# DeltaNet scan of a hybrid decoder layer: odd heads one chunk behind the even heads, two sides on opposite halves of the array

## The chip, the cores and the metric

The kernel runs on one core of one Trainium2 chip. A core has TensorE (PE, matrix products; PEld is its weight load), VectorE (DVE), ScalarE (ACT), GpSimd (POOL), SyncE (SP, whose queue issues most loads), a working memory with 128 partitions (rows), and eight accumulator banks (PSUM) that TensorE writes. A matmul that contracts over 64 partitions and writes 64 partitions uses one quarter of TensorE's array: the rows of the array follow the partitions that the operands are read from, its columns those that the result is written to. The metric is the device time of one execution in microseconds.

## What is computed

One decoder layer on 512 tokens with 1024 features, all in float32: normalise, one input projection, three groups of mixers side by side (gated DeltaNet, sparse attention, causal pooling), an output projection, then a squared-ReLU MLP. The change is in the DeltaNet's recurrence. Six heads of 64 features each carry a 64x64 state S over eight chunks of 64 tokens:

```
def step(S, xs):
    u_i, w_i, qk_i, qd_i, kd_i, gl_i = xs
    v_new = u_i - jnp.einsum('bhcd,bhde->bhce', w_i, S)
    o = jnp.einsum('bhcd,bhde->bhce', qd_i, S) + jnp.einsum('bhcs,bhse->bhce', qk_i, v_new)
    S = S * gl_i[..., None, None] + jnp.einsum('bhcd,bhce->bhde', kd_i, v_new)
    return S, o
```

`u` and `w` come from a triangular system per chunk, which the kernel inverts beforehand ("the solve").

## The kernel before

The 512 tokens lie in four tiles (index i) of 128 partitions, so each tile holds two chunks: chunk p=0 on partitions 0 to 63, chunk p=1 on 64 to 127 (`halves[p]`). Five generators are run side by side: `solves` (the systems of tiles 0 and 1 together, then of 2 and 3), `preps`, `slabs` (the input projection, the big 128x256 matmuls of L336), `compress` (L498 to L542) and `scans`. Each yields a cost, and the one that lags most emits next. A scheduler then puts the emitted instructions of each engine in a fixed order. Every engine works through its list in order; PE's list mixes the small matmuls of the solve and the scan with the big ones of the projection, later with attention scores (L983 to L985) and the output projection (L139 to L141 on `hwo`, `lwo`).

The solve (`gdn_solve`, matmuls in `sysmm`, L708) goes in legs: twelve matmuls of 64x64 on PE, one operation on VectorE or ScalarE (L729, L734, L737, later L744 to L762), and the next twelve need its result. `sysmm` alternates p=0 and p=1, so neighbours use opposite quarters of the array; both halves write one tile of one bank.

The scan (`gdn_scan`) takes one chunk per step, all six heads on the same 64 partitions h. A step is five groups of six matmuls: L776 (TT times v) and L779 (minus w times S) into one accumulator tile, L787 (keys times v_new) into the other half of it, and L792 twice (queries times S, QK times v_new). Between them stand L785 (DVE copies v_new), L783 (POOL scales the state), L788 (DVE adds to the new state) and L795 (ACT copies the output out). The scan's accumulator is bank 3 alone, so a step's first matmul comes after the copy of L795 of the step before. `S` is one tile whose half alternates. Steps of tiles 0 and 1 follow the first pair of solves, those of 2 and 3 the second. When all is done `gdn_out` normalises the tiles for the output projection (transposes at L812).

Of the kernel before, what the change touches and what calls it, by code (L numbers as in the profile page):

```python
# [9 lines left out]
F32 = mybir.dt.float32  # L10
# [6 lines left out]
ALU = mybir.AluOpType  # L17
# [20 lines left out]
def trunk_kernel(ctx, tc, x, norm_mix, w_in, conv_w, a_log, dt_bias, gdn_norm, nsa_q_norm, nsa_k_norm,  # L38
                 cmp_pos, cmp_w1, cmp_w2, pool_w, pool_scale, w_out, norm_ffn, w_ffn1, w_ffn2, out):
    nc = tc.nc  # L40
    V, S, G, PE, SY = nc.vector, nc.scalar, nc.gpsimd, nc.tensor, nc.sync
# [29 lines left out]
    pp_, ps_, pc_ = banks(3, 6), banks(3), banks(6)  # L71
# [137 lines left out]
    ps = pn()  # L209
# [401 lines left out]
    gs = gd.enter_context(pool("gs", 1))  # L611
    gte = ExitStack()
    gt = gte.enter_context(pool("gt", 1))
    St = gs.tile([P, H, HD], F32, tag="S", name="S")
    V.memset(St[0:64], 0.0)
    GB = dict(kT=2, D1=2, LT=4, QK=4, qdT=4, tmp=3, gls=1, vn=2, L16=4)
    for a in range(2):
        GB.update({f"X{a}": 1, f"IX{a}": 1, f"TT1{a}": 1, f"T{a}": 5, f"R{a}": 2})

# [5 lines left out]

    def w1t(shape, name, tag=None, dt=F32):
        tag = tag or name
        pl_ = gs if tag in ("LT", "QK", "qdT", "gls", "vn", "tmp") else gt
        return pl_.tile(shape, dt, tag=tag, name=nm(name), bufs=GB[tag])

    def hcol(s_):

        return 2 * (s_ % 3) + s_ // 3

    def v6(ps):
        return ps[:, 0:384].rearrange("p (s c) -> p s c", s=6)
# [132 lines left out]
    def gdn_scan(i):
        d = grp[i]  # L770
        o = vb[:, i]
        for p in range(2):
            h, nh = halves[p], halves[1 - p]
            ps = ps_()
            for s_ in range(6):
                PE.matmul(ps[h, ts(s_, HD)], d["TT"][h, s_], vb[h, i, hcol(s_)], start=(s_ == 0), stop=False,  # L776
                          skip_group_check=True)
            for s_ in range(6):
                PE.matmul(ps[h, ts(s_, HD)], kr[h, i, s_], St[h, hcol(s_)], start=False, stop=(s_ == 5),  # L779
                          skip_group_check=True)  # L780
            yield 0.8
            gls = w1t([P, H, HD], "gls")
            G.tensor_tensor(gls[h], St[h], egc[h, 2, i].unsqueeze(2).to_broadcast([64, H, HD]), ALU.mult)  # L783
            vn = w1t([P, 6, HD], "vn")
            V.tensor_copy(vn[h], v6(ps)[h])  # L785
            for s_ in range(6):
                PE.matmul(ps[nh, ts(hcol(s_), HD)], qr[h, i, hcol(s_)], vn[h, s_], start=True, stop=True)  # L787
            V.tensor_tensor(St[nh], v6(ps)[nh], gls[h], ALU.add)  # L788
            yield 0.4
            for a_ in range(2):  # L790
                for s_ in range(6):
                    PE.matmul(ps[h, ts(hcol(s_), HD)], (d["qdT"][h, s_ // 3, s_ % 3], d["QK"][h, s_])[a_],  # L792
                              (St[h, hcol(s_)], vn[h, s_])[a_], start=(s_ == 0 and a_ == 0), stop=(s_ == 5 and a_ == 1),
                              skip_group_check=True)
# [106 lines left out]

    def scans():
        yield from until("v")
        for ab in ((0, 1), (2, 3)):
            yield from until(ab)
            for i in ab:
                if i == 2:
                    y_tiles((0, 1, 2))
                yield from gdn_scan(i)
                have.add(("s", i))  # L910
# [377 lines left out]
```

## Time and profile before

| what | value |
|---|---|
| median of three runs | 753.72 us (753.46 to 754.56) |
| the profiled execution's own time | 756.4 us |
| span of its instructions | 754.2 us |
| PE busy in the span | 720.5 us (96%) |
| DVE busy | 550.1 us (73%) |
| ACT, POOL busy | 369.2 us, 216.7 us |
| scan, first to last matmul | 182.3 to 304 us of the span |

The profile is of one execution, whose own time is 2.2 us over its span and 2.7 us over the median. PE's busy time is modelled, so 96% busy doesn't say that it does useful work at its best rate for 96% of the time. A float32 matmul appears as two instructions in the trace, here called passes: six matmuls are 12 rows. The granted clock is given as a share of 2.4 GHz: 1.0 is the upper level, 0.5 the lower one of 1.2 GHz.

### The profile page before, as it was taken

The page shows a single profiled execution, that of the slowest core. Times are in us where ns is not written, and L with a number is a line of the kernel's source. Part 1 is how long each engine was busy: PE and PEld are TensorE (multiplying, and loading weights), DVE is VectorE, ACT ScalarE, POOL GpSimd, SP SyncE. Part 2 cuts the span into 40 slices and gives each one's busy share as a digit, 9 for nine tenths or more (in the row PEclk, how much of TensorE's full clock was granted, in tenths as well). Part 3 has the DMA queues.
Part 4 walks back from the last instruction along what each step waited for, and adds up shares of the span by engine and source line. Part 5 has one row for each costly group of instructions (what it writes and reads, how often), then busy time and mean ns, then how long its engine had stood idle before and what let it go on. Part 6 is the DMA issues. An engine that isn't in the chain of part 4 may idle for free.

```text
span 754.2 us, 13267 instructions
## 1 busy us (share of the span) xinstructions
PE 720.5 (96%) x5191; PEld 584.0 (77%) x5191; DVE 550.1 (73%) x1021; ACT 369.2 (49%) x724; POOL 216.7 (29%) x262
## 2 busy tenths in 40 slices
PE   3799989999999999999999999999999999999997
PEld 2788867798899887765557987878788888888886
DVE  5736997879786468667545599796868779686846
ACT  4445654456564235556644555454355444454440
POOL 8335354541514301000002042321405050412323
PEclk9599999999999989999999999999999999999999
DMA  8213321223211053003002042514233331413102
GB/s 268 74 32 84 84 64 45 63 72 104 76 54 30 21 215 102 29 29 118 23 1 85 1 143 81 168 56 141 83 113 111 94 130 44 129 52 112 56 0 111
DMA packets 49921, 62.19 MB, mean 82 GB/s; under 512 B 5494, under 2 KB 42564, under 8 KB 49860
## 3 DMA queue, kind: packets, MB, share of 16 engines
q1 hardware_dynamic: 48144, 60.95, 25.9%
q8 instruction: 40, 0.66, 0.4%
q10 hardware_dynamic: 1716, 0.41, 0.3%
q14 instruction: 21, 0.17, 0.1%
HBM read 59.25 MB, written 2.10 MB: 81 GB/s over the span
## 4 chain that ended last, share of the span: by engine, by line
PE 66%; DVE 21%; DMA 4%; issue 3%; ACT 3%; POOL 2%; SPq 0%; DVEq 0%; ACTq 0%; POOLq 0%
PE ps L139 14%; PE ps L140 14%; PE ps L141 13%; PE ps L336 5%; PE ps L1018 4%; DVE bl L1164 3%; DMA w2r<-in_w_ffn_dram 2%; PE ps L708 2%; DVE x L1257 2%; DVE lw L131 2%; PE ps L1007 2%; PE ps L792 1%; PE ps L983 1%; PE ps L984 1%; PE ps L498 1%
## 5 line engine op out<-in xcount | busy, mean ns | idle before, releaser
L140 PE MATMUL ps<-h2l,hw 128*128 128x512 f32 (+1 forms) x280 | 104.7, 374 | 0.1
L141 PE MATMUL ps<-h2h,lw 128*128 128x512 f32 (+1 forms) x280 | 104.7, 375 | 0.0
L139 PE MATMUL ps<-h2h,hw 128*128 128x512 f32 (+1 forms) x280 | 104.0, 374 | 0.0
L1171 POOL TENSOR_TENSOR al<-gF,ah 128x512 fp32r<-128x512 f32 x24 | 37.7, 1572 | 221.0 <-ACT ah L1170 182.4
L139 PE MATMUL ps<-bh,ah 128*128 128x512 f32 x224 | 88.5, 395 | 2.3 <-DVE x L1257 2.0
L140 PE MATMUL ps<-bl,ah 128*128 128x512 f32 x224 | 88.2, 394 | 0.0
L141 PE MATMUL ps<-bh,al 128*128 128x512 f32 x224 | 84.6, 393 | 0.0
L1257 DVE TENSOR_TENSOR x<-ps,x 128x512 f32<-128x512 f32 x112 | 72.7, 680 | 6.1 <-PE ps L141 5.9
L131 POOL TENSOR_TENSOR lo<-raw,hi 128x512 fp32r<-128x512 f32 (+2 forms) x45 | 60.1, 1349 | 53.5 <-ACT hi L130 49.0
L1164 DVE TENSOR_TENSOR bl<-w2r,bh 128x1024 fp32r<-128x1024 f32 x40 | 57.8, 1446 | 6.3 <-ACT bh L1163 6.3
L1171 POOL TENSOR_TENSOR al<-gS,ah 128x512 fp32r<-128x512 f32 x32 | 53.4, 1687 | 26.0 <-ACT ah L1170 24.7
L140 PEld LDWEIGHTS ps<-h2l,hw 128*128 128x128 f32 x280 | 52.6, 188 | 10.5 <-DVE h2l L1135 0.3
L141 PEld LDWEIGHTS ps<-h2h,lw 128*128 128x128 f32 x280 | 52.5, 188 | 10.2
L139 PEld LDWEIGHTS ps<-h2h,hw 128*128 128x128 f32 x280 | 52.3, 188 | 9.9
L130 ACT CAST hi<-raw 128x512 fp32r<-128x512 f32 (+2 forms) x78 | 39.6, 534 | 30.5 <-DMA raw<-in_w_in_dram 18.1
L1163 ACT CAST bh<-w2r 128x1024 fp32r<-128x1024 f32 x40 | 41.8, 1047 | 24.5 <-PE ps L141 23.5
L139 PEld LDWEIGHTS ps<-bh,ah 128*128 128x128 f32 x224 | 42.0, 188 | 13.5 <-issue 1.8
L141 PEld LDWEIGHTS ps<-bh,al 128*128 128x128 f32 x224 | 42.1, 188 | 9.8
L140 PEld LDWEIGHTS ps<-bl,ah 128*128 128x128 f32 x224 | 42.1, 188 | 9.6
L1170 ACT CAST ah<-gS 128x512 fp32r<-128x512 f32 x32 | 19.7, 620 | 51.6 <-DVE gS L1239 24.4
L131 DVE TENSOR_TENSOR lw<-raw,hw 128x1024 fp32r<-128x1024 f32 x32 | 41.2, 1320 | 4.3 <-ACT hw L130 4.3
L130 ACT CAST hw<-raw 128x1024 fp32r<-128x1024 f32 x32 | 32.1, 1046 | 22.6 <-PE ps L140 22.3
(346 smaller groups left out, 1737.5 us busy)
## 6 DMA issues: line engine op xcount, KB each, us to landing
raw<-in_w_ffn_dram SPq DMA_DIRECT2D x32, 512.0 KB, 4.0
w2r<-in_w_ffn_dram SPq DMA_DIRECT2D x32, 512.0 KB, 5.4
raw<-in_w_in_dram SPq DMA_DIRECT2D x24, 256.0 KB, 2.8
raw<-in_w_in_dram SPq DMA_DIRECT2D x36, 128.0 KB, 2.3
x<-in_x_dram SPq DMA_DIRECT2D x8, 512.0 KB, 5.4
raw<-in_cmp_w_dram SPq DMA_DIRECT2D x32, 128.0 KB, 2.2
raw<-in_w_out_dram SPq DMA_DIRECT2D x8, 512.0 KB, 3.6
out_dram<-x SPq DMA_DIRECT2D x8, 256.0 KB, 2.0
```

The lines of the kernel that those rows point to most:

```text
L130: {"A": S.copy, "V": V.tensor_copy, "G": G.tensor_copy}[e[0]](hi[:, k], r)
L131: {"V": V, "G": G}[e[1]].tensor_tensor(lo[:, k], r, f32v(hi[:, k]), ALU.subtract)
L139: PE.matmul(ps, ah, bh, start=start, stop=False, **kw)
L140: PE.matmul(ps, ah, bl, start=False, stop=False, **kw)
L141: PE.matmul(ps, al, bh, start=False, stop=stop, **kw)
L336: PE.matmul(ps[:, ts(i, 256)], a_[:, k, ts(2 * b + i, P)], w_, start=(k == 0 and n_ == 0 and i == 0), stop=(k == KC - 1 and n_ == 2 and i ...
L1018: PE.matmul(acc[halves[a], i * P:(i + m) * P], Vt[k // 2][:, k % 2, 2 * br + h // 3, :], pt[:, c * P:(c + m) * P], start=False, stop=(br = ...
L1163: S.copy(hi, src)
L1164: V.tensor_tensor(lo, src, f32v(hi), ALU.subtract)
L1170: S.copy(hi, src)
L1171: G.tensor_tensor(lo, src, f32v(hi), ALU.subtract)
L1257: V.tensor_tensor(x2[i][:, cs], acc[bk, t_], x2[i][:, cs], ALU.add)
```

## The change

`gdn_step` takes the place of `gdn_scan`. There are nine steps in place of eight. In step t the even heads (three of them) work on chunk t and the odd heads on chunk t-1, so that the even ones read and write partitions `halves[p]` and the odd ones the other half. Step 0 has the even side alone and step 8 the odd side alone. Within each of the five groups the two sides alternate, matmul by matmul. VectorE's copy and add work on both sides at once: 128 partitions by 192 in place of 64 by 384. POOL's scaling and ScalarE's copy-out are one instruction per side, 64 by 192 each. The state is a new tile each step (three buffers), and the update part of a step stands in columns 192 to 383 of the accumulator tile. The last step updates no state. Step 4 needs the second pair of solves, as the fifth chunk did before, and the odd heads' fourth chunk is in that step too.

```diff
-    St = gs.tile([P, H, HD], F32, tag="S", name="S")
-    V.memset(St[0:64], 0.0)
-    GB = dict(kT=2, D1=2, LT=4, QK=4, qdT=4, tmp=3, gls=1, vn=2, L16=4)
+    GB = dict(kT=2, D1=2, LT=4, QK=4, qdT=4, tmp=3, gls=2, vn=2, S=3, L16=4)
...
+    def gdn_step(t, St):
+
+        sides = []
+        for a in range(2):
+            if 0 <= t - a < 2 * NT:
+                i, p = divmod(t - a, 2)
+                sides.append((grp[i], i, halves[p], halves[1 - p], 3 * a, slice(a, H, 2)))
+        rows, nrows = (slice(0, P), slice(0, P)) if len(sides) == 2 else sides[0][2:4]
+        ps = ps_()
+        p3 = ps[:, 0:384].rearrange("p (a s c) -> p a s c", a=2, s=3)
+        for j in range(3):
+            for d, i, h, nh, s0, hs in sides:
+                PE.matmul(ps[h, ts(j, HD)], d["TT"][h, s0 + j], vb[h, i, hcol(s0 + j)], start=(j == 0), stop=False,
...
+        for j in range(3):
+            for d, i, h, nh, s0, hs in sides:
+                PE.matmul(ps[h, ts(j, HD)], kr[h, i, s0 + j], St[h, j], start=False, stop=(j == 2),
...
+        vn = w1t([P, 3, HD], "vn")
+        V.tensor_copy(vn[rows], p3[rows, 0])
...
+            for d, i, h, nh, s0, hs in sides:
+                G.tensor_tensor(gls[nh], St[h], egc[h, 2, i, hs].unsqueeze(2).to_broadcast([64, 3, HD]), ALU.mult)
+            for j in range(3):
+                for d, i, h, nh, s0, hs in sides:
+                    PE.matmul(ps[nh, 192 + HD * j:192 + HD * j + HD], qr[h, i, hcol(s0 + j)], vn[h, j], start=True, stop=True)
...
+            V.tensor_tensor(Sn[nrows], p3[nrows, 1], gls[nrows], ALU.add)
...
+        for d, i, h, nh, s0, hs in sides:
+            S.copy(vb[h, i, hs], p3[h, 0])
+        yield 0.4
+        return Sn
...
+        St = w1t([P, 3, HD], "S")
+        V.memset(St, 0.0)
+        for t in range(2 * NT + 1):
+            yield from until((0, 1) if t < 4 else (2, 3))
+            if t == 4:
+                y_tiles((0, 1, 2))
+            St = yield from gdn_step(t, St)
```

The lines of the changed file differ: L779, L783, L796 and L804 are the five groups of matmuls there, L787 the copy of v_new, L799 the add; L706 is the solve's L708, and after the scan a line is 14 higher (L997 is L983, L1021 is L1007, L1032 is L1018).

First place: PE's list at the last step but one of the scan, which stands among the attention's matmuls (scores L983 to L985, transposes L1007, values L1018). Before, that is the last chunk of all six heads:

```order
L776 MATMUL ps_3420<-vb,LT_1368 64x64 x6
L779 MATMUL ps_3420<-S,kr 64x64 x6
L983 MATMUL ps_4714<-XT_4088,XT_3582 128x128
L984 MATMUL ps_4714<-XT_4089,XT_3582 128x128
L1018 MATMUL ps_4561<-pt_4641,Vt_4025 64x512
L1018 MATMUL ps_4561<-pt_4681,Vt_4025 64x384
L1018 MATMUL ps_4561<-pt_4681,Vt_4027 64x128
L1007 MATMUL ps_4699<-ident,P_4609 128x128
L1007 MATMUL ps_4699<-ident,P_4617 128x128
L985 LDWEIGHTS identb
L985 MATMUL ps_4714<-negb,identb 128x128
L787 MATMUL ps_3420<-vn_3435,qr 64x64 x6
```

After, the same place has step 7; the first two rows are of step 6, where the two sides are on different tiles, so that their alternation can be seen in the names (`LT_1366` is tile 3's, `LT_1331` tile 2's):

```order
L779 MATMUL ps_3385<-vb,LT_1366 64x64
L779 MATMUL ps_3385<-vb,LT_1331 64x64
...
L779 MATMUL ps_3425<-vb,LT_1366 64x64 x6
L783 MATMUL ps_3425<-S_3401,kr 64x64 x6
L997 MATMUL ps_4824<-XT_4112,XT_3613 128x128
L998 MATMUL ps_4824<-XT_4113,XT_3613 128x128
L999 LDWEIGHTS identb
L999 MATMUL ps_4824<-negb,identb 128x128
L1032 MATMUL ps_4585<-pt_4751,Vt_4049 64x512
L1021 MATMUL ps_4809<-ident,P_4690 128x128
...
L796 MATMUL ps_3425<-vn_3438,qr 64x64 x6
```

A two-sided step has as many matmuls as a step had before; what changed is that neighbours in a group belong to different sides.

Second place: PE's list at the end of the second pair of solves, where `ps_2993` and `ps_3012` are the two systems' last residuals and L336 is the input projection. Before:

```order
L708 MATMUL ps_2993<-X_2848,LT_1333 64x64 x12
L708 LDWEIGHTS R_2886
L708 MATMUL ps_2964<-TT_2830,R_2886 64x64
...
L708 LDWEIGHTS R_2992
L708 MATMUL ps_3032<-TT_2961,R_2992 64x64
...
L708 MATMUL ps_3012<-X_2882,LT_1368 64x64 x12
L336 MATMUL ps_4240<-hi_4241,hTh 128x256
```

After (`ps_2991` and `ps_3010` are the same residuals):

```order
L706 MATMUL ps_2991<-X_2846,LT_1331 64x64 x12
L336 MATMUL ps_4263<-hi_4323,hTl 128x256
...
L706 MATMUL ps_2962<-TT_2828,R_2884 64x64
...
L706 MATMUL ps_3030<-TT_2959,R_2990 64x64
...
L336 MATMUL ps_4264<-hi_4265,hTh 128x256
...
L336 MATMUL ps_4264<-hi_4323,hTh 128x256
L706 MATMUL ps_3010<-X_2880,LT_1366 64x64 x12
L706 MATMUL ps_3080<-LT_1331,kr 64x64 x12
```

Before, 24 matmuls of the solve and nothing else stand between the two residuals; now 13 matmuls of L336 stand ahead of them and 25 behind, inside the chain.

Third place: PE's list at one leg of the second pair of solves, during the second step of the scan. `T,L` is a leg's first product, whose result VectorE takes (L729), and `TT,W` needs that. Before:

```order
L708 MATMUL ps_2332<-T_2256,L_1359 64x64
L498 MATMUL ps_2694<-hi_2904,fs_1926 128x256
L498 MATMUL ps_2694<-lo_2905,fs_1926 128x256
L498 MATMUL ps_2694<-hi_2983,fs_1926 128x256
L461 MATMUL ps_3815<-ident,X_3761 128x128
L336 MATMUL ps_3852<-hi_3935,hTl 128x256
...
L461 MATMUL ps_3815<-ident,X_3762 128x128
L787 MATMUL ps_3167<-vn_3182,qr 64x64 x4
L498 MATMUL ps_2694<-lo_2984,fs_1926 128x256
L787 MATMUL ps_3167<-vn_3182,qr 64x64 x2
L708 LDWEIGHTS W_2227
L708 MATMUL ps_2316<-TT_2193,W_2227 64x64
```

After:

```order
L706 MATMUL ps_2330<-T_2254,L_1357 64x64
L498 MATMUL ps_2692<-hi_2693,fs_1924 128x256
L498 MATMUL ps_2692<-lo_2694,fs_1924 128x256
L498 MATMUL ps_2692<-hi_2802,fs_1924 128x256
L498 MATMUL ps_2692<-lo_2803,fs_1924 128x256
L804 MATMUL ps_3154<-S_3140,qdT_1260 64x64 x6
L804 MATMUL ps_3154<-vn_3167,QK_1269 64x64 x4
L706 LDWEIGHTS W_2225
L706 MATMUL ps_2314<-TT_2191,W_2225 64x64
```

The stretch that covers VectorE's part of the leg lost seven matmuls of L336 and two transposes, and got ten of the scan in place of six.

## Rows read from the trace of the kernel before

**Rows 1.** The page: busy time, share of the span and instructions of each engine.

```profile
PE 720.5 (96%) x5191; PEld 584.0 (77%) x5191; DVE 550.1 (73%) x1021; ACT 369.2 (49%) x724; POOL 216.7 (29%) x262
```

**Rows 2.** Busy time of each engine in stretches of 10 us from the scan's first step to the end of the second solves: stretch, its length, then busy us and instructions of PE, PEld, DVE, ACT, POOL, the granted clock, DMA's share and GB/s.

```profile
180.00:190.00 10.00, 9.95 (x211) 9.24 (x208) 9.77 (x38) 5.55 (x16) 2.30 (x4) 1.00 0.21 62
...
210.00:220.00 10.00, 9.87 (x175) 9.11 (x171) 9.44 (x35) 6.63 (x17) 1.00 (x1) 1.00 0.26 71
...
240.00:250.00 10.00, 8.25 (x175) 7.49 (x172) 7.69 (x16) 4.18 (x9) 0.79 (x3) 0.99 0.01 2
sum 70.00, PE 67.51 PEld 62.11 DVE 55.06 ACT 39.20 POOL 23.17; mean PE 9.64 PEld 8.87 DVE 7.87 ACT 5.60 POOL 3.31
```

**Rows 3.** The same view in stretches of 2 us, at the end of the second solves and 16 us later.

```profile
246.00:248.00 2.00, 0.67 (x26) 0.52 (x20) 1.94 (x5) 1.11 (x4) 0.00 (x0) 1.00 0.00 0
248.00:250.00 2.00, 1.57 (x37) 1.32 (x38) 1.94 (x6) 1.15 (x3) 0.26 (x1) 0.94 0.00 0
250.00:252.00 2.00, 2.00 (x10) 2.00 (x10) 1.52 (x3) 0.00 (x0) 2.00 (x5) 0.50 0.03 8
252.00:254.00 2.00, 2.00 (x28) 1.87 (x27) 0.00 (x0) 0.00 (x0) 2.00 (x4) 0.71 0.00 0
266.00:268.00 2.00, 2.00 (x25) 1.97 (x25) 1.23 (x1) 1.16 (x2) 0.00 (x0) 0.71 1.02 418
268.00:270.00 2.00, 2.00 (x11) 1.78 (x10) 1.53 (x2) 0.00 (x0) 0.00 (x0) 0.50 1.03 416
270.00:272.00 2.00, 2.00 (x6) 1.61 (x5) 1.50 (x5) 0.34 (x1) 0.00 (x0) 0.50 1.05 412
272.00:274.00 2.00, 2.00 (x14) 1.25 (x14) 0.96 (x3) 0.18 (x1) 0.00 (x0) 0.59 0.62 246
```

**Rows 4.** The timeline of PE at the scan's last chunk: start, us from the first pass's start to the last one's modelled end, line, operation, tiles, shape, passes. What a group takes of PE is its start to the next row's start.

```profile
294.65 0.91 PE L776 MATMUL ps<-vb,LT 64*64 64x64 f32 x12
295.39 0.86 PE L779 MATMUL ps<-S,kr 64*64 64x64 f32 x12
296.19 0.33 PE L983 MATMUL ps<-XT,XT 128*128 128x128 f32 x1
...
298.84 0.91 PE L787 MATMUL ps<-vn,qr 64*64 64x64 f32 x12
299.68 0.39 PE L983 MATMUL ps<-XT,XT 128*128 128x256 f32 x1
...
302.25 0.91 PE L792 MATMUL ps<-S,qdT 64*64 64x64 f32 x12
303.00 0.86 PE L792 MATMUL ps<-vn,QK 64*64 64x64 f32 x12
303.79 0.50 PE L983 MATMUL ps<-XT,XT 128*128 128x512 f32 x1
```

**Rows 5.** The same view at the end of the first solves, where float32 matmuls of the solve alternate between opposite quarters of the array and write both halves of one bank; and at a preparation step (L651), where all read the same 64 partitions and the result alternates between the halves.

```profile
121.88 0.72 PE L651 MATMUL ps<-qT,kT 64*64 64x64 f32 x23
...
180.85 0.92 PE L708 MATMUL ps<-X,LT 64*64 64x64 f32 x24
181.59 0.87 PE L708 MATMUL ps<-LT,kr 64*64 64x64 f32 x24
182.29 0.28 PE L776 MATMUL ps<-vb,LT 64*64 64x64 f32 x2
```

**Rows 6.** The scan's passes of L776 in the whole span, and the operations of other engines in a step, then the nearest rows of the new shapes, by line: engine, operation, tiles, count, ns shortest/median/longest, first and last start.

```profile
L776 PE MATMUL ps<-vb,LT x96: 218/218/298, 182.3 to 295.3; 64*64 64x64 f32 x96
L785 DVE COPY vn<-ps x8: 539/556/561, 185.2 to 296.9; 64x384 f32<-64x384 f32 x8
L788 DVE TENSOR_TENSOR S<-ps,gls x8: 550/556/561, 187.5 to 300.3; 64x384 f32<-64x384 f32 x8
L783 POOL TENSOR_TENSOR gls<-S,egc x8: 824/830/1869, 53.4 to 286.2; 64x384 f32<-64x384 f32 x8
L795 ACT COPY vb<-ps x8: 472/474/477, 193.6 to 303.9; 64x384 f32<-64x384 f32 x8
L654 DVE TENSOR_TENSOR QK<-ps,D x8: 342/350/358, 123.1 to 158.8; 128x192 f32<-128x192 f32 x8
L696 ACT COPY qdT<-ps x16: 302/314/317, 118.6 to 155.9; 64x192 f32<-64x192 f32 x16
L661 POOL TENSOR_TENSOR gU<-g,le x8: 507/520/959, 48.2 to 137.5; 128x192 f32<-128x192 f32 x8
```

**Rows 7.** The timeline of all engines at the leg of the third place above (`T,L` on PE, VectorE's queue, `TT,W` on PE).

```profile
197.76 0.35 PE L708 MATMUL ps<-T,L 64*64 64x64 f16 x12
197.82 1.16 DVE L131 TENSOR_TENSOR lo<-raw,hi 128x256 fp32r<-128x256 f32 x1
...
198.05 0.39 PE L498 MATMUL ps<-hi,fs 128*128 128x256 f32 x1
...
199.01 0.56 DVE L729 CAST_PREDICATED W<-lv,ps 128x384 f16<-128x384 uint16 x1
...
200.58 0.28 PE L708 MATMUL ps<-TT,W 64*64 64x64 f16 x6
```

**Rows 8.** Who waited for whom, PE alone, 170 to 330 us: line, releaser, us in total, times, longest.

```profile
PE ps L708 <- DVE R L746: 1.4, 1, 1.4
PE ps L533 <- ACT kx L528: 0.6, 1, 0.6
```

More of the change, by code (lines that the diff above doesn't have):

```diff
@@ L627, in w1t @@
         tag = tag or name
-        pl_ = gs if tag in ("LT", "QK", "qdT", "gls", "vn", "tmp") else gt
+        pl_ = gs if tag in ("LT", "QK", "qdT", "gls", "vn", "S", "tmp") else gt
         return pl_.tile(shape, dt, tag=tag, name=nm(name), bufs=GB[tag])
@@ L767, in gdn_solve @@
         yield 0.8
[L769 to L776, printed above, removed]
+    def gdn_step(t, St):
[10 more added lines that the diff above has]
+                PE.matmul(ps[h, ts(j, HD)], d["TT"][h, s0 + j], vb[h, i, hcol(s0 + j)], start=(j == 0), stop=False,
@@ L777, in gdn_scan @@
                           skip_group_check=True)
-            for s_ in range(6):
-                PE.matmul(ps[h, ts(s_, HD)], kr[h, i, s_], St[h, hcol(s_)], start=False, stop=(s_ == 5),
+        for j in range(3):
+            for d, i, h, nh, s0, hs in sides:
+                PE.matmul(ps[h, ts(j, HD)], kr[h, i, s0 + j], St[h, j], start=False, stop=(j == 2),
                           skip_group_check=True)
-            yield 0.8
-            gls = w1t([P, H, HD], "gls")
-            G.tensor_tensor(gls[h], St[h], egc[h, 2, i].unsqueeze(2).to_broadcast([64, H, HD]), ALU.mult)
@@ L784, in gdn_scan @@
[L784 to L793, printed above, removed]
+        yield 0.4
@@ new lines, in gdn_step @@
+        vn = w1t([P, 3, HD], "vn")
+        V.tensor_copy(vn[rows], p3[rows, 0])
+        Sn = St
+        if t < 2 * NT:
+            gls = w1t([P, 3, HD], "gls")
+            Sn = w1t([P, 3, HD], "S")
+            for d, i, h, nh, s0, hs in sides:
[3 more added lines that the diff above has]
+                    PE.matmul(ps[nh, 192 + HD * j:192 + HD * j + HD], qr[h, i, hcol(s0 + j)], vn[h, j], start=True, stop=True)
+            if t == 0:
+                V.memset(Sn[sides[0][2]], 0.0)
+            V.tensor_tensor(Sn[nrows], p3[nrows, 1], gls[nrows], ALU.add)
+            yield 0.2
@@ L794, in gdn_scan @@
+        for a_ in range(2):
+            for j in range(3):
+                for d, i, h, nh, s0, hs in sides:
+                    PE.matmul(ps[h, ts(j, HD)], (d["qdT"][h, s0 // 3, j], d["QK"][h, s0 + j])[a_],
+                              (St[h, j], vn[h, j])[a_], start=(j == 0 and a_ == 0), stop=(j == 2 and a_ == 1),
                               skip_group_check=True)
-            S.copy(o[h], v6(ps)[h])
-            yield 0.8
+        for d, i, h, nh, s0, hs in sides:
+            S.copy(vb[h, i, hs], p3[h, 0])
@@ L798, in gdn_out @@
+        yield 0.4
+        return Sn
     def gdn_out(i):
@@ L903, in scans @@
         yield from until("v")
[L904 to L910, printed above, removed]
+        St = w1t([P, 3, HD], "S")
[5 more added lines that the diff above has]
+            St = yield from gdn_step(t, St)
     def compress():
```

## The prediction

> **What bounds the kernel now.** I read the page first: PE is busy for 720.5 of 754.2 us, so a change pays if it takes work or gaps off PE, and little otherwise [rows 1]. Busy time is modelled, so I then asked in what stretch the scan lies and whether PE waits there. From 180 to 250 us PE is busy for 67.51 of 70 us and VectorE for 55.06; VectorE is the next in line, POOL (23.17) and ACT (39.20) are far off [rows 2]. The view of waits, 170 to 330 us, has two waits of PE above half a microsecond [rows 8]. What is not full is one spot: 246 to 250 us, where PE is busy for 0.67 and 1.57 of 2 us while VectorE has 1.94 twice. That is the end of the second solves, a chain of short legs with nothing to fill it. Right behind it PE's granted clock is 0.50 and 0.71, and again 0.71 to 0.50 at 266 to 274 us, with PE busy throughout [rows 3]. So in this stage PE's own work sets the time, and I cost the change by what it does to that.
>
> **The pairs, the main term.** In the timeline of the last chunk a group of twelve passes takes 295.39 - 294.65 = 0.74 us (L776), 0.80 (L779), 0.84 (L787), 0.75 and 0.79 (L792), together 3.92 us a step [rows 4]. That is about 62 ns a pass, plus 0.18 us a step where a group is followed by another shape. Eight steps of twelve passes a group, 96 of L776 in all [rows 6], are 31.4 us. The solve has passes of the same shape, float32 64x64, whose neighbours use opposite quarters: 24 passes take 181.59 - 180.85 = 0.74 us, the next 24 take 0.70, so 30 ns each [rows 5]. The changed groups L779, L783 and L804 are of that pattern, each on its side's own quarter. The group L796 crosses: the even side reads one half and writes the other, the odd side the reverse. No row has that; the nearest is L651, with both on the same rows and opposite columns, 23 passes within 0.72 us, at most 31 ns [rows 5]. At worst L796 gains nothing and costs 0.84, which is 0.37 a step, 2.6 us over seven steps; I take the paired price and keep that end.
>
> So a two-sided step is 60 passes at 30.8 ns, 1.85, plus the same 0.18: 2.03 us. Step 0 has 30 passes at 62 ns plus 0.18, 2.04 us. Step 8 has no state update, 24 passes, 1.58 us. Seven times 2.03 plus these is 17.8 us. **31.4 - 17.8 = 13.6 us less on PE.** All of it lies on PE, which is full around it.
>
> One rule speaks against it. The rows show that products from the two row halves write one bank and still run at 30 ns a pass, since `sysmm` writes one tile [rows 5]. The Trainium skill (TensorEngine Tiling (Array Packing), Restrictions and Gotchas) says that different row tiles write different PSUM banks and cannot access one bank at the same time. Both sides here write bank 3, so by that rule this term would be about nothing. The trace disagrees for two halves of one bank, and I go by the trace.
>
> **The other engines.** VectorE's copy and add were 0.556 us each, sixteen of them, 8.9 us. They become seventeen of 128x192 or 64x192; the nearest row, the 128x192 product of L654 out of PSUM, is 0.35, so 5.9 us [rows 6]: 3.0 less on an engine that is off the path as long as PE is full. ACT gets 16 copies of 64x192 at 0.314 (row of L696) for eight at 0.474, 5.0 for 3.8 us. POOL gets 15 scalings, between half of 0.83 and the 0.52 of L661, about 7.1 for 6.6 us. Both lie beside PE's work on engines with room. POOL's two in a row are wanted by the add, which must wait for L796 anyway; if they were last, a step would be late by about 0.1 us. The two memsets stand before the scan.
>
> **The gap and the clock.** The idle time at 246 to 250 us is 1.33 + 0.43 = 1.76 us. The low clock behind it costs 0.12 + 1.00 + 0.58 = 1.70 us, that at 266 to 274 us 0.58 + 1.00 + 1.00 + 0.82 = 3.40 us, each being the share of the stretch not granted [rows 3]. The order shows 25 matmuls of the projection now inside the chain that had none (second place), so VectorE's part of it has cover. But these matmuls are the ones that stood behind the chain, so a later leg loses them. I take half of 1.76 + 1.70, **1.7 us**, and keep 0 and 3.5 as ends. For the second dip there is no wait to remove; the run of small products in which it fell gets shorter by a scan step's share, so I take half again, **1.7 us**, with 0 and 3.4 as ends.
>
> **New waits.** What covers a solve's leg gets thinner. In the third place VectorE's result came at 199.01 + 0.56 = 199.57, PE took it at 200.58: a slack of 1.0 us [rows 7], bought by 2.5 us of other work. After, that cover is four L498 and ten scan matmuls. From the leg's end at 198.11 VectorE needed 1.46 us, 0.56 of it the operation and the rest its queue (an L131 of 1.16 stood ahead). Twenty passes at 31 ns are 0.6 us and the four L498 at least the 0.39 of the first one here, so PE waits there between nothing (a shorter queue) and 0.5 us. By the order three legs between steps 1 and 3 are so thin; the others keep some 2 us. Step 1 follows step 0 closely and needs bank 3, hence ACT's copy of 0.31 us and its queue: up to 0.5 us. The extra ninth step lies among attention work, where PE has other matmuls ready. Altogether I charge **2.5 us**; the ends are 0 and, if VectorE paces the whole first half, 15.7 - (2.04 + 3 x 2.03) = 7.6 us, all that four steps save.
>
> **Sum.** -13.6 - 1.7 - 1.7 + 2.5 = -14.5 us. Against the profiled execution, 756.4, that is 741.9. The median of the runs is 2.7 us lower, so the forecast is 753.7 - 14.5 = **739.2 us**. Ends: -13.6 - 3.5 - 3.4 = -20.5, 733.2; and -13.6 + 7.6 = -6.0, 747.7. The untaken end of L796 lies inside.
>
> **Rivals.** *The pairs don't overlap* (the rule above, or accumulating chains that behave unlike the solve's single products). For: no row has an accumulating pair. Against: rows 5. PE's work is then 474 passes in place of 480, 0.4 us less, plus a ninth step's hand-overs: 753.7, give or take 1.5. Chance 0.05.
>
> *VectorE becomes the bound of the first half.* It had 55.06 of 70 us [rows 2]; the four steps spare it about 1.5. If PE's 70 us shrink by 7.6 and the gap's 3.5 to 59, VectorE is at 53.6 of 59, 91%, in a queue that works in order and holds results of the solve behind splits (L131). Then the first half saves nothing and only the four steps or so behind it do: 747.7 to 752, 750 say. For: 9.77 and 9.44 of 10 us in two stretches already. Against: in just these PE was full as well. Chance 0.08.
>
> *Slower, by the clock.* The dip at 266 us came with PE busy 2.00 of 2.00 [rows 3], so it takes no idle time. If thinner cover leaves PE with short pauses between small products all along the solves and the scan, the granted clock can be 0.5 for long stretches there, from 182 to 304 us. Each such microsecond costs half of one; the 13.6 us are gone from 27 us more at the lower level, and at 40 us the result is 753.7 - 13.6 + 20 = 760. For: the dips exist. Against: in the stretches of legs shown the clock was 0.99 to 1.00 [rows 2]. Chance 0.05.
>
> **Chances.** The forecast has 0.82. Two kernels within 0.2%, 1.5 us, can't be told apart by this measurement. Faster by more: forecast, the VectorE rival and a little of the first, 0.91; within 0.2%: most of the first, 0.03; slower: the clock and what is left, 0.06. The range 733 to 748 holds the forecast with its ends and leaves out the rivals.
>
> **What would show it.** In the changed profile a two-sided group of twelve passes should take 0.37 to 0.45 us of PE, start to next start; L796 tells whether crossing pairs overlap. L787 and L799 on VectorE should be near 0.35 us. PE's gap at the end of the second solves should be mostly gone and the clock behind it 1.0. The scan's last matmul should come some 14 us earlier than 304. If the groups are at 0.37 and the time is not down, the loss must show as waits of PE at L706 for L727 (L729 before), or as a granted clock under 1.0; if the groups are still at 0.75, the first rival holds.

## The result, and the profile after

The changed kernel takes 747.21 us, median of four runs (745.59 to 748.27), beside 754.14 us for the kernel before: a ratio of 0.9907, interval 0.9889 to 0.9926. Six more runs of it (e0 below) gave 0.9882, 0.9857 to 0.9906. So it is 7 to 9 us faster. The forecast was 14.5 us less, 739.2: the sign and the range held, the size was half. (Two executions of e10, its profiled one among them, at a granted clock of 0.56 and 0.75, and one of e1, at 1370 us, are slow ones and stand in no ratio or median below; e12 is e10's kernel again.)

The two profiled executions differ by more, 754.2 to 743.9 us of span. Of these 10.3 us, 2.0 lie ahead of the scan, whose first matmul starts at 182.29 before and 180.33 after. That is not the change: PE's list ahead of it is the same, instruction by instruction, in both kernels and in e0, e1, e5 and e7 below, whose scans start at 180.3, 181.2, 180.3 and 182.1 us. The granted clock differs there: at 30 to 40 us it was 0.76 before and 1.00 after. From the scan's first matmul to the end it is 571.9 and 563.6 us, 8.3 less, near what the runs show. In the view of busy times (columns as in [rows 2]), before, then after:

```profile
182.29:754.18 571.89, 561.00 (x3690) 449.89 (x3686) 414.33 (x712) 272.80 (x509) 131.13 (x119) 0.99 0.25 80
```

```profile
180.33:743.88 563.55, 549.11 (x3684) 435.94 (x3680) 408.54 (x712) 275.01 (x517) 129.35 (x125) 0.99 0.25 81
```

There PE is busy for 11.9 us less and idle for 14.4 us in place of 10.9.

The page's first line, PE's and VectorE's part of it against [rows 1], 13 and 7 us of busy time less:

```profile
PE 707.5 (95%) x5185; PEld 568.4 (76%) x5185; DVE 543.1 (73%) x1023; ACT 371.6 (50%) x732; POOL 215.1 (29%) x269
```

PE's timeline at step 7, the last two-sided step (columns as in [rows 4]; its L779 and L783 answer to L776 and L779 there, L796 to L787, L804 to L792):

```profile
289.86 0.56 PE L779 MATMUL ps<-vb,LT 64*64 64x64 f32 x12
290.25 0.52 PE L783 MATMUL ps<-S,kr 64*64 64x64 f32 x12
...
293.52 0.56 PE L796 MATMUL ps<-vn,qr 64*64 64x64 f32 x12
...
295.72 0.57 PE L804 MATMUL ps<-S,qdT 64*64 64x64 f32 x12
296.12 0.52 PE L804 MATMUL ps<-vn,QK 64*64 64x64 f32 x12
```

The starts give 0.39 us for L779 (290.25 - 289.86) and 0.40 for the first L804, 33 ns a pass; 0.74 and 0.75 before [rows 4]. From start to next start over the whole scan, the groups sum to 19.4 us (L779 3.5, L783 4.1, L796 4.0, L804 7.8) against 31.0 before (5.7, 6.9, 6.4, 12.0). The pairs took 11.6 us off PE in these two executions. Passes that fell into stretches at a granted clock of 0.50 make 1.0 of the 31.0 us and 0.2 of the 19.4, so at an equal clock it is 30.0 and 19.2, 10.8 us less.

The stretch beside the second solves, from the scan's first matmul to the first one of the fifth chunk, in one row of the view of busy times (columns as in [rows 2]); the kernel before, then after:

```profile
182.29:254.53 72.24, 69.81 (x1186) 64.52 (x1183) 54.58 (x172) 37.06 (x93) 27.70 (x38) 0.98 0.18 47
```

```profile
180.33:249.35 69.02, 63.98 (x1152) 58.24 (x1149) 49.41 (x156) 36.75 (x95) 27.60 (x40) 0.98 0.19 49
```

PE is busy for 5.8 us less, but idle for 5.0 in place of 2.4, so this stretch is only 3.2 us shorter. (It has 210 of the scan's passes in place of 240: the odd heads' fourth chunk is now in the step behind it.) What follows, from there to the end, is 5.1 us shorter (499.6 to 494.5).

Who waited for whom, PE alone, 170 to 330 us, as in [rows 8]:

```profile
PE ps L706 <- DVE W L727: 1.3, 2, 1.0
PE ps L533 <- DVE kx L530: 0.9, 1, 0.9
PE ps L498 <- ACT hi L130: 0.8, 1, 0.8
PE ps L139 <- DVE x L1099: 0.7, 1, 0.7
PE ps L336 <- DVE zt L584: 0.6, 1, 0.6
PE ps L533 <- ACT kx L528: 0.6, 1, 0.6
PE ps L498 <- DVE lo L131: 0.4, 1, 0.4
PE ps L796 <- DVE vn L787: 0.2, 1, 0.2
```

Before there were three, the two of [rows 8] and 0.3 us at L336; now there are eight. Only the first is at a leg of the solve; L533 and L498 belong to `compress`, which PE's list mixes in: L498 multiplies by weights that L130 and L131 split, L533 transposes the compressed key. The timeline of VectorE, ACT and PE shows the largest:

```profile
186.25 0.68 DVE L449 TENSOR_TENSOR qks<-ps,r 128x512 f32<-128x512 f32 x1
...
187.41 0.38 PE L706 MATMUL ps<-TT,W 64*64 64x64 f16 x12
...
188.11 0.24 ACT L528 CAST kx<-kcs 64x64 fp32r<-64x64 f32 x1
...
188.40 0.27 PE L533 MATMUL ps<-ident,kx 64*128 64x64 f32 x1 [0.61 <-ACT kx L528]
...
188.80 0.75 DVE L530 TENSOR_TENSOR kx<-kcs,kx 64x64 f32<-64x64 f32 x1
...
189.61 0.27 PE L533 MATMUL ps<-ident,kx 64*128 64x64 f32 x1 [0.94 <-DVE kx L530]
```

PE stands at L533 until 189.61. In the kernel before, 22 matmuls of L336 stand between the scan's first matmul and L533; here there are none, and they come behind it.

The same stretch in slices of 2 us, with that of the second solves' end (244) and the second dip (258 to 264), against [rows 3]:

```profile
186.00:188.00 2.00, 1.51 (x62) 1.36 (x59) 1.80 (x7) 1.44 (x5) 0.90 (x2) 1.00 0.00 0
188.00:190.00 2.00, 0.66 (x4) 0.46 (x5) 1.76 (x4) 1.59 (x6) 1.41 (x2) 1.00 0.02 4
190.00:192.00 2.00, 2.00 (x21) 1.75 (x21) 1.86 (x9) 0.18 (x1) 0.00 (x0) 0.68 0.00 0
192.00:194.00 2.00, 2.00 (x30) 1.71 (x30) 1.76 (x10) 0.48 (x1) 0.92 (x2) 0.50 0.04 8
194.00:196.00 2.00, 1.51 (x47) 1.27 (x46) 0.95 (x2) 0.87 (x3) 1.39 (x4) 0.97 0.00 0
...
244.00:246.00 2.00, 1.36 (x16) 1.29 (x11) 1.97 (x6) 0.72 (x2) 1.26 (x4) 1.00 0.00 0
...
258.00:260.00 2.00, 2.00 (x29) 1.84 (x30) 1.45 (x2) 1.76 (x4) 0.00 (x0) 0.74 1.05 422
260.00:262.00 2.00, 2.00 (x7) 1.40 (x7) 2.00 (x4) 0.81 (x2) 0.00 (x0) 0.50 1.02 408
262.00:264.00 2.00, 2.00 (x9) 1.43 (x7) 1.90 (x11) 0.53 (x1) 0.00 (x0) 0.90 1.00 395
```

The idle time at the end of the second solves is 0.64 us in place of 1.76, and the clock behind it 1.00. But where PE was idle for 1.8 us (186 to 190) the granted clock then falls to 0.50, as it did at 250 us before. In all the share not granted costs 0.64 + 1.00 + 0.06 + 0.52 + 1.00 + 0.20 = 3.4 us, against 5.1 before [rows 3].

### The profile page after: what moved, and what is told of

Same layout as the page of the kernel before. It is cut to its first block, busy times and chain, and to the rows that moved or that the text cites. A ratio compares the mean times of both kernels' runs of the same rounds, so it can differ in the third digit from the quotient of the medians.

```text
span 743.9 us, 13280 instructions
## 1 busy us (share of the span) xinstructions
PE 707.5 (95%) x5185; PEld 568.4 (76%) x5185; DVE 543.1 (73%) x1023; ACT 371.6 (50%) x732; POOL 215.1 (29%) x269
## 3 DMA queue, kind: packets, MB, share of 16 engines
q1 hardware_dynamic: 48144, 60.95, 26.3%
## 4 chain that ended last, share of the span: by engine, by line
PE 54%; DVE 11%; issue 3%; DMA 3%; ACT 3%; POOL 0%; SPq 0%; DVEq 0%; ACTq 0%; POOLq 0%
PE ps L139 13%; PE ps L140 13%; PE ps L141 13%; PE ps L1032 4%; PE ps L336 3%; PE ps L1021 2%; DMA raw<-in_w_out_dram 2%; DVE bl L1178 2%; DVE x L1271 2%; PE ps L997 1%; DVE lw L131 1%; PE ps L706 1%; PE ps L998 1%; DMA w2r<-in_w_ffn_dram 1%; DVE gS L1251 1%
## 5 line engine op out<-in xcount | busy, mean ns | idle before, releaser
L139 PE MATMUL ps<-h2h,hw 128*128 128x512 f32 (+1 forms) x280 | 104.0, 374 | 0.0
L1185 POOL TENSOR_TENSOR al<-gF,ah 128x512 fp32r<-128x512 f32 x24 | 34.4, 1433 | 228.4 <-ACT ah L1184 189.6
L139 PE MATMUL ps<-bh,ah 128*128 128x512 f32 x224 | 88.4, 394 | 0.9 <-DVE x L1271 0.9
L131 POOL TENSOR_TENSOR lo<-raw,hi 128x512 fp32r<-128x512 f32 (+2 forms) x45 | 60.4, 1358 | 57.0 <-ACT hi L130 53.4
L140 PEld LDWEIGHTS ps<-h2l,hw 128*128 128x128 f32 x280 | 52.6, 188 | 10.3 <-DVE h2l L1149 0.3
L141 PEld LDWEIGHTS ps<-h2h,lw 128*128 128x128 f32 x280 | 52.5, 188 | 10.3
L139 PEld LDWEIGHTS ps<-h2h,hw 128*128 128x128 f32 x280 | 52.3, 188 | 9.8
L130 ACT CAST hi<-raw 128x512 fp32r<-128x512 f32 (+2 forms) x78 | 39.4, 534 | 27.2 <-DMA raw<-in_w_in_dram 15.6
L139 PEld LDWEIGHTS ps<-bh,ah 128*128 128x128 f32 x224 | 42.0, 188 | 11.8 <-ACT ah L1184 0.8
L131 DVE TENSOR_TENSOR lw<-raw,hw 128x1024 fp32r<-128x1024 f32 x32 | 39.0, 1254 | 7.8 <-ACT hw L130 7.6
L130 ACT CAST hw<-raw 128x1024 fp32r<-128x1024 f32 x32 | 32.2, 1048 | 23.7 <-PE ps L140 22.8
L139 PE MATMUL ps<-hTh,hi 128*128 128x512 f32 x104 | 42.6, 410 | 0.0
```

The lines of the kernel that those rows point to most:

```text
L130: {"A": S.copy, "V": V.tensor_copy, "G": G.tensor_copy}[e[0]](hi[:, k], r)
L131: {"V": V, "G": G}[e[1]].tensor_tensor(lo[:, k], r, f32v(hi[:, k]), ALU.subtract)
L139: PE.matmul(ps, ah, bh, start=start, stop=False, **kw)
L140: PE.matmul(ps, ah, bl, start=False, stop=False, **kw)
L141: PE.matmul(ps, al, bh, start=False, stop=stop, **kw)
L1185: G.tensor_tensor(lo, src, f32v(hi), ALU.subtract)
```

## The experiments

Theory: beside the second solves the scan's passes are the work that covers the solve's and the compression's results; what the pairs save there comes partly back as waits. Rivals: the pairs save less than they seem; another engine sets the pace there; the granted clock takes it; any new list differs by that much.

**e0, the changed kernel again** (no edit).

> The changed kernel once more, five rounds, to see its spread and a second profile. Theory (cover): the waits of PE at the scan's first two steps (about 2 us between 183.8 and 190 us: L706 for L727, L533 for kx) are there in every execution, because PE's list is fixed; time 747 us, within 1.5. Rival (clock): the profiled execution's dip at 190.71 to 194.12 us is chance, and what differs between executions is how many stretches of 3.4 us at 0.50 there are; then the waits are there, the dip at 190 us is not, and dips stand elsewhere.

Measured: 746.71 us (745.64 to 747.83), ratio 0.9882. The profiled execution has the same eight waits to a tenth, a ninth of 0.2 us, and its clock at 0.5 from 190.5 to 193.9 and 258.8 to 262.2. So the waits belong to the list. The dip at 190 us came again, which speaks against the rival, on two executions.

**e1, side after side; e4, side after side over whole phases.** In e1 the loops over sides and matmuls are exchanged in each group; in e4 a side does two groups before the other starts.

```diff
-        for j in range(3):                          # e1, in each of the five groups
-            for d, i, h, nh, s0, hs in sides:
+        for d, i, h, nh, s0, hs in sides:
+            for j in range(3):
...
+        for d, i, h, nh, s0, hs in sides:           # e4: L779 and L783 in one loop over sides, L804 likewise
+            for j in range(3):
+                PE.matmul(ps[h, ts(j, HD)], d["TT"][h, s0 + j], vb[h, i, hcol(s0 + j)], start=(j == 0), stop=False,
...
+            for j in range(3):
+                PE.matmul(ps[h, ts(j, HD)], kr[h, i, s0 + j], St[h, j], start=False, stop=(j == 2),
```

> The changed kernel, but within each group all matmuls of the even side come first and then those of the odd side, so neighbours share a quarter of the array. PE's list is otherwise nearly the same, and so are the other engines' instructions. Theory (pairs worth their full term, something else gives back): a two-sided step goes from 2.2 us back to 3.9, seven of them 11.8 us, less about 1 us because longer scan groups cover some waits: 747 + 11 = 758, slower than the kernel before by some 4 us. Rival (the pairs are worth no more than the 7 us measured): 754. Rival (the order of the side in the group does not matter to the array): 747.

> The changed kernel with the sides as the outermost loop of each phase: twelve passes of L779 and L783 of the even side, then twelve of the odd side; L796 six and six; L804 twelve and twelve. When each group was written side after side (run e1), the trace had the odd side's first pass start 0.17 us after the even side's first, while three of the even side's six were still to come, at 58 ns a pass on each side. Theory (PE reaches some three passes ahead into another quarter, no further): 9 + 12 passes at 58 ns, 1.22 us, for each of the two long phases and 0.66 for L796, 3.1 us a step against 2.2, seven times 0.9 = 6.5 us more on PE. By the worth of PE's time that e1 gave here (5.5 us more on PE cost 2.9 us) that is 3.4: 750. Rival (PE's time is worth its full length here): 753. Rival (the order is free over whole phases): 2.2 us a step, 747.

e1: 749.26 us, 2.5 more than e0, measured beside it, where 11 were expected. The reason is in PE's timeline of e1 at step 7, where the list has twelve passes of L779, then twelve of L783, each the even side's six first:

```profile
291.64 0.61 PE L779 MATMUL ps<-vb,LT 64*64 64x64 f32 x10
292.04 0.22 PE L783 MATMUL ps<-S,kr 64*64 64x64 f32 x1
292.09 0.22 PE L779 MATMUL ps<-vb,LT 64*64 64x64 f32 x1
292.10 0.22 PE L783 MATMUL ps<-S,kr 64*64 64x64 f32 x1
292.15 0.22 PE L779 MATMUL ps<-vb,LT 64*64 64x64 f32 x1
292.16 0.56 PE L783 MATMUL ps<-S,kr 64*64 64x64 f32 x10
```

Passes of L783 start ahead of passes of L779 that precede them in the list. PE reaches ahead into another quarter, so most of the overlap comes without alternation: both groups take 1.01 us here (292.65, the next row's start, less 291.64), 0.84 alternating, 1.5 before. My estimate of e1 took the overlap to be the alternation's; that was wrong. e1 has 24.9 us of scan passes, 24.0 at an equal clock, which is 4.8 more than the changed kernel, and is 2.5 us slower.

e4: 750.99 us, where by the same theory 750 was expected. A long phase takes 1.36 us (two of them and L796's 0.66 make 3.4 a step), so the reach is some three passes. Its profiled execution, 6.5 us over its median, has 28.7 us of scan passes, of which 2.4 are clock not granted; the other 26.3 are some 7 more than in e0, and they cost about 4 us. In both kernels some two fifths to a half of the extra PE time costs nothing, and the waits shrink with it. The waits of PE in e4, 180 to 255 us, are 1.8 us in all; the changed kernel has 4.6 there.

```profile
PE ps L533 <- DVE kx L530: 0.9, 1, 0.9
PE ps L336 <- DVE zt L584: 0.6, 1, 0.6
PE ps L706 <- DVE W L727: 0.3, 1, 0.3
```

**e8 and e9, each half of the change alone.** `gdn_scan` is kept for one half of the chunks and `gdn_step` used for the other.

```diff
+        for i in range(2):                      # e8
+            yield from gdn_scan(i, S6)
...
+        for t in range(4, 9):
+            yield from gdn_step(t, St, 4, 8, t == 8)
...
+        for t in range(5):                      # e9
+            yield from gdn_step(t, St, 0, 4, False)
...
+        for i in range(2, 4):
+            yield from gdn_scan(i, S6)
```

> Half of the change: chunks 0 to 3 as in the kernel before (all six heads on one half of the array), chunks 4 to 7 in two-sided steps (one step with the even side alone, three with both, one with the odd side alone). Theory (beside the second solves, scan time taken off PE comes back as waits; beside the attention it does not): most of the gain is in this half, 5 us: 749.5, while the first half alone (run e9) gives 2 to 3. Rival (the scan's passes are worth the same everywhere): 3.7 us each, 750.5 for both. Rival (the second half is worth nothing, its waits being those of the attention): 754.

> The other half of the change: chunks 0 to 3 in two-sided steps (five steps, the last with the odd side alone), chunks 4 to 7 as in the kernel before. Two copies on POOL bring the state together. Theory (as for e8): 2 to 3 us faster than the kernel before, 751.5. Rival (worth the same everywhere): 750.5. Rival (the first half is worth its full 6 us of PE's time): 748.

e8: 750.67 us against 754.87, 4.2 faster (ratio 0.9951, 0.9928 to 0.9973). e9: 753.98, 0.9 faster (0.9991, 0.9967 to 1.0015). So more of the gain is in the half beside the attention, as expected, though the intervals, 2.0 to 5.4 us faster and 2.5 faster to 1.1 slower, overlap. The first half gave less than the 2 to 3 us of the theory. The halves don't add up to the whole: each has three two-sided steps, the change seven. The waits of PE, 180 to 255 us, in e8 are the kernel before's, 2.3 us, while its scan takes 5.1 us less of PE at an equal clock (24.9 for 30.0):

```profile
PE ps L706 <- DVE R L744: 1.4, 1, 1.4
PE ps L533 <- ACT kx L528: 0.6, 1, 0.6
PE ps L336 <- DVE zt L584: 0.3, 1, 0.3
```

and in e9, with only this half paired, 5.8 us in all, 3.5 more, while its scan takes 3.9 us less (26.1 at an equal clock):

```profile
PE ps L706 <- DVE W L727: 2.3, 3, 1.1
PE ps L533 <- DVE kx L530: 0.9, 1, 0.9
PE ps L498 <- ACT hi L130: 0.9, 1, 0.9
PE ps L706 <- DVE R L744: 0.8, 1, 0.8
PE ps L533 <- ACT kx L528: 0.6, 1, 0.6
...
```

**e2 and e3, the projection earlier; e5 and e6, a shorter chain to L533; e7, kx on POOL.** Each gives the changed kernel (e2, e5, e7) or the kernel before (e3, e6) cover or a shorter wait at 184 to 190 us. e5 and e6 leave out the normalisation of the compressed key.

```diff
-    side_by_side((90, solves()), (100, preps()), (102.0, slabs()), (10, compress()), (80, scans()))
+    side_by_side((90, solves()), (100, preps()), (108, slabs()), (10, compress()), (80, scans()))     # e2, e3
...
-            rsqrt(r[0:64], ss[0:64], 1, 64)
+            V.tensor_copy(r[0:64], ss[0:64])                                                          # e5, e6
...
-            V.tensor_tensor(kx[:, 1, 0:HD], kcs, kx[:, 0, 0:HD], ALU.subtract)
+            G.tensor_tensor(kx[:, 1, 0:HD], kcs, kx[:, 0, 0:HD], ALU.subtract)                        # e7, both halves
```

> The changed kernel with the projection's track given weight 108 in place of 102, which puts 1.9 and 1.1 us of L336 between the legs of the scan's steps 0 and 1, where the changed kernel has none, and before L533. Theory (cover): PE's waits between 183.8 and 190 us (2.0 us) go, and with them the clock's dip right behind (1.7 us): 747.2 - 3.7 = 743.5. Rival (the loss is elsewhere, or the dip comes with any run of small products): 746 to 748. Rival (an earlier projection delays the solves): over 748.

> The kernel before with the same weight 108 for the projection's track. Theory (cover): the kernel before has 2.8 us of L336 there already, so nothing is to be won at the scan's start; the idle time at the end of the second solves may go, 1.8 us plus the dip behind it: 750 to 754. Rival (weight 108 is simply better for both): as much faster as the changed kernel gets, 3.7 us, 750.

> The changed kernel without the reciprocal square root of the compressed key's norm, so that key is not normalised: a dozen VectorE operations on one column fewer in the chain that L533 waits for. Theory (cover): the waits at L533 (1.5 us) go, and the legs beside them wait less: 2 to 3 us faster, 744.5. Rival (PE then waits as long for the next result of the solve's chain): within 1 us of 747.

> The kernel before with the same operations left out. Theory (cover): its wait there was 0.6 us, so 0 to 1 us faster, 753 to 754.5. Rival (a shorter chain is worth the same in both kernels): 2 to 3 us faster, 751.5.

> The changed kernel with the two subtractions of kx (L529, L530, 0.64 and 0.75 us on VectorE) on POOL, which is idle there; the second L533 then stands behind two L336. Theory (VectorE's queue is what PE waits for at 184 to 198 us): 1 us or more faster, 745.5. Rival (POOL's longer operation only moves the wait): 746.5 to 748.

Measured: e2 754.29, e3 763.93; e5 750.32, e6 758.74; e7 749.56 us. All five came out slower than the kernel they edit, by 2 to 9 us; the theory's gains of up to 4 us were misses. In e2 the waits at L533 and L498 shrink as expected (0.7 us is left), but the scan starts at 189.1 us, 6.8 later than in the kernel before: the list lost ahead of the scan what it won in it. In e5 and e7 waits grow at other lines (L804 for L799 1.7 us, new in e5; L706 for L727 from 1.3 to 2.3 in e7). A small edit moves PE's whole list, and the time with it by more than the wait in question. The change's own worth is steadier: e3 less e2 is 9.6 us, e6 less e5 8.4.

**e10 to e15, four buffers for the split weights of the compression; e16 and e17, buffers of its own for its second part.** e11 and e17 are the kernel before with the same edit, e12 is e10 again, e13 is e4 with it, e14 and e15 are e10 with one weight of the planner changed (10 to 8, 102 to 100).

```diff
-            hi, lo = load_half([(0, cmp_w1[0, a, r0:r0 + P, :])], "c", (4, 2, 1), "AV")
+            hi, lo = load_half([(0, cmp_w1[0, a, r0:r0 + P, :])], "c", (4, 4, 1), "AV")                            # e10 to e15
+            hi, lo = load_half([(0, cmp_w1[0, a, r0:r0 + P, :])], "cd"[a], ((4, 2, 1), (2, 4, 1))[a], "AV")       # e16, e17
```

> The changed kernel with four buffers in place of two for the split weights of the compression (the tiles hi and lo that L498 reads). PE's list then has 1.7 and 2.4 us between the legs of the scan's first steps, L498 among it, and L533 two legs earlier. Theory (the new waits are the compression's, L498 for L130 and L131, 1.7 us, and L533 for kx, 1.5 us): 2 to 4 us faster, 743.5. Rival (any new list moves the waits to other places): 746 to 751, as in the runs e2, e5 and e7.

> The kernel before with the same four buffers. Theory (these waits are the changed kernel's): 0 to 1 us faster, 753.5. Rival (a list with more room is better for both): 2 to 4 us faster, 751. Rival (any new list is worse than the one in place): over 756.

> The kernel of e10 once more, whose profile fell on an execution at a granted clock of 0.56 throughout. Its times were 744.8 to 745.2 us where the clock was 0.993 and 748.7 to 750.8 where it was 0.979 to 0.988. Theory (cover): in the profile, PE's waits above 0.3 us between the scan's start and the end of the second solves are under 3 us, against 5.9 in the changed kernel, with none at L533 or L498; the time goes with the granted clock as before, 745 to 750. Rival (waits only move): 5 us of waits or more, at other lines.

> The kernel of e10 with the sides as the outermost loop of each phase, as in e4: 8.4 us more of PE's time in the scan. In the list with two buffers that cost 4.3 us. Theory (PE's time in the scan is worth its length where the legs are covered): 8 us more than e10, 757. Rival (half, whatever the list, since another engine paces the first half): 4 us more, 753.5.

> The kernel of e10 with weight 8 in place of 10 for the compression's track, which leaves the legs' cover about as it is. Theory (cover): 745 to 750, as e10. Rival (the place in the list decides, not the cover): more than 2 us off e10, either way.

> The kernel of e10 with weight 100 in place of 102 for the projection's track, cover of the legs slightly thinner. Theory (cover): 746 to 751. Rival (the place in the list decides): more than 2 us off e10, either way.

> The changed kernel with buffers of their own for the weights of the compression's second part (two raw, four split), the first part's as they were. PE's list ahead of the scan is then nearly that of the changed kernel, and the legs of the scan's first steps have 2.4 to 2.6 us of L336 between them, L533 three legs later. Theory (cover): the waits at L533 and L498, 3.3 us, go, and nothing is lost ahead of the scan, which e10 lost: 743.5, faster than both kernels. Rival (the waits move to other lines, as in e2, e5 and e7): 747 or more.

> The kernel before with the same buffers. Theory (cover): the change is worth 11 to 14 us where the changed kernel's legs are covered, so 754 to 757 here. Rival (the change is worth 7 to 8 us in any list): 750.5 to 751.5, 7 to 8 more than e16.

Medians: e10 749.39 (ratio 0.9911), e11 763.09 (1.0107), e12 748.28 (0.9897), e13 757.51 (1.0020), e14 749.70, e15 748.33, e16 748.57 (0.9913), e17 755.79 (0.9995). None beats the changed kernel; e14 and e15, with the legs' cover about as in e10, are within 2 us of e10, as the theory had it. e10 was a miss (743.5 expected), e11 too: it fits the rival that a new list is worse than the one in place. e12 has 3.4 us of such waits, 1.1 of them at L533 and L498, where under 3 and none there were expected. e13 came at the 757 of its theory. e11 less e10, measured beside it, is 13.7 us and e17 less e16 7.2: what the change is worth depends on the list, and over five lists it is 7 to 14 us. The stretch from the scan's first matmul to the fifth chunk's, by the view of busy times:

| kernel | length | PE busy | PE idle | clock |
|---|---|---|---|---|
| before | 72.24 | 69.81 | 2.43 | 0.98 |
| e11 (four buffers, before) | 75.75 | 71.08 | 4.67 | 0.95 |
| e4 | 72.73 | 70.67 | 2.06 | 0.91 |
| e1 | 69.23 | 66.12 | 3.11 | 0.95 |
| after | 69.02 | 63.98 | 5.04 | 0.98 |
| e13 (four buffers, by phase) | 68.58 | 65.16 | 3.42 | 0.98 |
| e12 (four buffers) | 65.08 | 61.74 | 3.34 | 0.97 |
| e17 (own buffers, before) | 70.09 | 66.75 | 3.34 | 0.98 |
| e16 (own buffers, after) | 69.73 | 61.46 | 8.27 | 1.00 |

A lower clock makes PE's busy time longer, so the rows of e4, e1 and e11 don't compare in length with the others.

With four buffers, e13's 3.4 us more of PE's work make the stretch 3.5 us longer and the whole kernel 9.2: there PE's time is worth its full length. So in that list no other engine sets the pace as such, and VectorE, busy for 49.4 of 69.0 us in the changed kernel, isn't full. But those lists lose ahead of the scan what they win in it: it starts at 183.6 to 188.2 us in e12 to e15. e17 fell within its theory's 754 to 757, but with e16 where it is, the change's 7.2 us there are what the rival said. e16 was a miss: with 2.4 to 2.6 us of L336 between the first legs, where the changed kernel has none, PE is idle for 8.3 us. The waits are at later legs and at L498, the largest sums of that view (180 to 255 us) being

```profile
PE ps L498 <- ACT hi L130: 1.6, 3, 0.7
PE ps L706 <- ACT TT L735: 1.3, 2, 0.9
PE ps L706 <- DVE W L727: 1.1, 2, 0.9
PE ps L498 <- DVE lo L131: 1.0, 1, 1.0
```

So what the pairs save in this stretch is worth nearly nothing in one list (e17 to e16: 5.3 busy us less, some 1.4 of them by the clock, and 0.4 us of length), half in another (before to after: 5.8 and 3.2), all in a third (e13 to e12, where only the order of the sides was changed: 3.4 and 3.5). In these runs the length of the work between two legs did not tell which of it a list gives.

## Why the prediction was half right

Two terms of the sum were mis-sized, and they make most of the difference: the pairs, taken at 13.6 us, brought 10.8, and the new waits, charged at 2.5 us, are 4.6. The second failed in kind too.

- **The pairs: right in kind, 2.8 us too high.** Two-sided groups overlap, also the crossing L796, and the first rival is out. The sum took 13.6 us off PE; 11.6 came off, 10.8 at an equal clock. The kernel before had 30.0 at that clock, not 31.4: eight times the last chunk was too much. A two-sided step has 0.39 us in L779, 0.40 in the first L804, 0.45 in L783 and the second L804, 0.50 in L796: 2.18 us, not 2.03, 1.1 us in seven steps. L796 costs more by its neighbours and not by crossing: its last pass starts 0.347 us after its first, in L779 0.346; from there to the next start it is 0.15 us, as behind L783, since another shape follows. The other 0.3 us were not told apart. The rule of the Trainium skill (TensorEngine Tiling (Array Packing), Restrictions and Gotchas), that different row tiles can't be in one PSUM bank at once, is not what the trace shows: both halves write bank 3 at 33 ns a pass.
- **VectorE, ACT, POOL: right.** The copy and the add take 0.350 and 0.354 us, as the row of L654 said, the copy-out 0.314 and POOL's scaling 0.508:

```profile
L787 DVE COPY vn<-ps x9: 341/350/361, 183.0 to 299.1; 128x192 f32<-128x192 f32 x7, 64x192 f32<-64x192 f32 x2
...
L799 DVE TENSOR_TENSOR S<-ps,gls x8: 344/354/361, 184.4 to 294.2; 128x192 f32<-128x192 f32 x7, 64x192 f32<-64x192 f32 x1
```

- **The gap and the clock: about right in sum.** 3.4 us were taken; the gap gave 1.1 and the clock 1.7. The dip behind the gap went, but another came behind the new idle time at 188 us, which the prediction had only as a rival with a chance of 0.05 and at another scale.
- **New waits: the step that failed.** "Altogether I charge 2.5 us." From the scan on PE is idle for 3.5 us more, although the gap gives back 1.1, so the new waits are 4.6 us, 2.1 more than charged. They lie inside the end of 7.6; the value taken did not hold. The step looked at legs of the solve (L706 for L727: 1.3 us, as described) and nowhere else. Of the 4.3 us that the view of waits names as new (the table's 5.5 less 0.6 at L533, which was there before, and less 0.6 at L336, what is left of the gap), 2.1 are the compression's (L533, L498) and 0.9 stand among the attention (L139, L796). These lines were in the list between the legs, and their own inputs were never priced. The other 0.3 us are too short for that view. So of the 6.2 us between the forecast's 14.5 and the 8.3 of the two executions, 2.8 are the pairs' size, 2.1 these waits and 0.6 the gap and the clock; 0.7 stay open. e9 bears this out: what its scan took less of PE came back as waits.
- **The VectorE rival: right place, wrong engine.** It said that the first half saves nothing and only the steps behind it do, 747.7 to 752. e8 and e9 give nearly this split, 4.2 and 0.9 us. But VectorE's share is 72% there, and e13 shows that PE's time can be worth its full length in this stretch. The waits point to the order of PE's list against several engines' results as what paces it; no run isolates that.
- **The end of the scan.** Its last matmul was to come some 14 us earlier than 304; the trace has it at 304. The planner filled the room with attention and projection work, so the place of the last step says nothing about the gain.
- **From the profile to the median.** The sum was made against one execution and taken off the median. The 2.0 us ahead of the scan, which are not the change's, would have been counted as a gain by a comparison of spans alone.

What stays open: which property of a list decides whether the first half's savings are kept (e12 keeps them, e16 doesn't), and how to keep them without losing time ahead of the scan. No version faster than the changed kernel was found.

## What to carry to other kernels

Price the work that a change takes away twice: once as time of the full engine, once as cover for whatever is mixed into its list there, and for the second look at the inputs of every line between the waits, not only at the chain you think of. Where an engine is 97% busy in a stretch that is a chain of short legs, take the saved time at its length only in the stretches beside independent work. In the chain it was worth anything from nearly nothing to all of it here, half in the changed kernel. When a scheduler orders the list, one small edit can move the time by several us; compare an edit in both kernels before calling it a cause.

## What the runs showed of the hardware

- PE starts matmuls of another quarter ahead of matmuls that stand before them in its list, some three passes far (e1: L783 at 292.04 us ahead of L779 at 292.09; in e4 the odd side's L779 starts when nine of the even side's twelve passes have started). So "every engine works through its list in order" holds for PE only within a quarter here. The Trainium skill (TensorE: Matmul & The Clock Gate, The mechanism) says that matmuls start strictly in program order and only weight loads are pulled ahead; this trace shows otherwise. By that rule e1 would have run near the kernel before; it was 5 us faster.
- Float32 passes of 64x64 on one quarter start 58 ns apart (L776 before). In pairs on opposite halves, into one bank, the two of a pair start 7 ns apart and the pairs 58 ns apart (L779 after), so 12 passes take 0.39 us in place of 0.74. Pairs that read one half and write the other keep the same pace (L796).
- The granted clock fell to 0.50 for 3.4 us right behind the idle time at 186 to 190 us in both executions of the changed kernel, as behind that at 246 to 250 us before. Idle time alone doesn't decide it: in e16 PE was idle for 8.3 us of its stretch and the clock stayed at 1.00, and e8, whose waits there are the kernel before's, was at 0.50 for 13.7 us from 191.1 us on.
